# A weight pool of three buffers kept open to the end, and two projection weights taken into an earlier stream of weights

## The chip, the cores and the metric

The kernel runs on one core of one Trainium2 chip, as a single launch. The metric is its device time in microseconds (us), as the median of several runs. In the profile, PE is TensorE (PEld its weight loads), DVE is VectorE, ACT is ScalarE, POOL is GpSimd, and SP is SyncE, which here only issues DMAs. The "granted clock" is the share of TensorE's full clock that its throttle granted.

## The reference

One layer of a hybrid encoder block is applied to 1024 tokens (one prompt and one sample of 512 each), with a model width of 1024, all in float32:

```python
h    = rms_norm(x, norm_g)
proj = h @ w_in      # [cq 384 | ckv 256 | k_rope 64 | gate_a 1024 | conv_in 2*1024 | gate_c 1024 | mg_a 1024 | mg_c 1024]
# branch A: latent attention, 8 heads, 128 plain + 64 rotary dimensions per head
q    = rms_norm(cq) @ w_uq;  k_nope, v = split(rms_norm(ckv) @ w_ukv)
q, k = per-head rms_norm, rotary on the last 64
y_a  = (softmax(q k^T / sqrt(192)) v * silu(gate_a)) @ w_o_attn
# branch C: convolution
u    = conv_in[:, :1024] * sigmoid(conv_in[:, 1024:])
u    = depthwise_conv31(u) + dw_bias
u    = silu(layer_norm(u)) * silu(gate_c)
y_c  = u @ w_pw2     # the pointwise projection
out  = x + (sigmoid(mg_a) * y_a + sigmoid(mg_c) * y_c) @ w_out
```

## The kernel before

Activations lie transposed: the 128 partitions hold 128 channels, the free dimension holds tokens, in two halves of 512. The tokens' halves are the two groups of a PSUM block (128 x 1024).

**Weights as two parts.** Each float32 matmul is done as three matmuls in the faster type fp32r: high part by high part, high weight by low activation, low weight by high activation. So each weight block of 1024 x 128 (stored as 128 x 1024) goes through `load` (L112, a 512 KB DMA into a buffer `raw`, issued on SP) and `split` (L117): ACT casts it into `whi` (L128), and `whi` is subtracted from it into `wlo` (L129) by DVE or by POOL. Weights have running numbers: `raw46`, `whi46` and `wlo46` belong to weight 46, which is p0, the first block of the pointwise projection.

**Buffers.** Weights of the first part live in the pool `w1` with three buffers each of `raw`, `whi` and `wlo`, and so a new split waits until PE has read the one three before for the last time, and until that one's `wlo` has been made (which frees `raw`). The same pool holds four work tiles `s1` to `s4`. At L586 the pool is closed and a new one, `w`, is opened with two buffers each of `whi` and `wlo`, and one of `raw`.

**Order.** The program hands out instructions to the engines by priorities and buffers. PE's own order is written out in code in the first part. Each engine runs its instructions in the order it was handed, and each waits for semaphores of others; so what stands ahead of a waiting instruction on an engine delays it. Weights are prepared ahead, at a raised priority, by two functions. In the first part it is `ensure` (L162), which runs along a list `stream`: a block that is entry e of it calls `ensure(e + 3)`, so that three entries are prepared when it starts, and its low part is made on POOL:

```python
e = used[0]
ensure(e + 3)
ps = [one_bank(f"i{e}_{b}") for b in range(2)]
block_mm(ps, stream[e][0], hh, hl, (0, 1), ks=range(4))
between()
block_mm(ps, stream[e][0], hh, hl, (0, 1), ks=range(4, KD))
```

After that it is `prep` (L182), with the low part on DVE: `block(i)` (L331) does block i and then calls `prep(i + 2)`.

**Stages in order of time.** (1) 0 to 50 us: x is loaded, normalised and transposed into `hH`/`hL`. (2) to 434 us: most blocks of `h @ w_in`, in pairs with fewer products, while DVE does the depthwise convolution. (3) to 504 us, the tail: the last six gate blocks ga2 to ga7 (entries 72 to 77 of the stream, weights 40 to 45; PSUM tile `pbi`). Among them run the "tokens": eight groups of 128 tokens, each with a load of the convolution's output `yt` and of the saved gate `gt` (SP), eight transposes (PE), statistics and the inverse deviation `lrs` (DVE, the power on POOL, L248), the normalised `z` (DVE, L552), eight transposes of z (PE, L558), the activation `zs` (ACT, L561), a product with the gate (DVE), a cast into `cH` (ACT, L564) and the low part `cL` (DVE, L565). Each gate block is finished by `gate_out` (L479): two ACT instructions from PSUM into `stga` (L482), and a DMA issued on ACT. The code of the tail and of what follows it:

```python
tail = plan[len(plan) - NLN :]
with tc.manual_schedule(engines={nc.tensor.engine}):
    take(*tail[0], single())
    for n, u in enumerate(tail[1:]):
        tokens(2 * n)
        take(*u, single(lambda: tokens(2 * n + 1)))
```

(4) 507 to 594 us: the pointwise projection, blocks p0 to p7 (weights 46 to 53), on `cH`/`cL` as activations; DVE multiplies each by a saved gate `smc` (L608). (5) the latents (weights 54 to 58), the rotary key (59) and rotary weights (60), then the merge gates ma6 and ma7 (61 and 63) and the weights of the heads (h0 is 62, h1 64, h2 65 and so on). ma6 and ma7 end in `late_gate` (L858): two ACT instructions `stma` (L861), in front of the first of which ACT loads another function table. (6) to 977 us: attention, by heads. The weights of the second rotary group (`rawr1`, high part `wrh` at L976, low part `wrl` at L977) are loaded in the first heads. The first head's key goes through the casts `kh` (L794, low part `kl` on DVE) and `k1`/`k2` (L803), its query through `qsq` (L771) and `qh`, its rotary part through `qr` (L704) and `qrT` (L718). (7) to 1064 us: `w_o_attn`, blocks o0 to o7, merged with the saved gates `sma` (L1030), which `load_merge` (L1016) loads. (8) to the end: `w_out`, and y is written.

Of the kernel before, what the change touches and what calls it, by code (L numbers as in the profile page):

```python
# [9 lines left out]
F32 = mybir.dt.float32  # L10
# [7 lines left out]
P = 128  # L18
D = 1024
S = 512  # L20
NT = 1024
KD = 8
# [5 lines left out]
TAPS = 31  # L28
# [15 lines left out]
def encoder_block(tc, xp_d, xs_d, win_d, wkr_d, whd_d, wqr_d, wo_d, wp_d, wout_d, vec_d, dwk_d, rg_d, rc_d, yp_d, ys_d):  # L44
# [3 lines left out]
    def open_pool(name, **kw):  # L48
        if kw.get("space") is not DRAM:
            kw["reuse_waits"] = "tile"  # L50
        cm = tc.tile_pool(name=name, **kw)
        opened[name] = cm
        return cm.__enter__()

    def close_pool(*names):
        for name in names:
            opened.pop(name).__exit__(None, None, None)

    f = lambda ap: ap.bitcast(F32)
# [11 lines left out]

    cp = open_pool("const", bufs=1, side="left")
    wp = open_pool("w1", bufs=3, side="left")
    dr = open_pool("dr", bufs=1, space=DRAM)

    ep = open_pool("edge", bufs=1, side="right")
# [4 lines left out]
    p1 = open_pool("p1", bufs=2, space=PSUM)  # L81

    vec = cp.tile([P, NV], F32, name="vec")
    dwk = cp.tile([P, KD, TAPS], F32, name="dwk")
    rt = cp.tile([P, 4, 4, RD], F32, name="rt")
    identf = cp.tile([P, P], F32, name="identf")
    identr = cp.tile([P, P], F32R, name="identr")
# [1 line left out]
    fold = cp.tile([P, RD], F32, name="fold")  # L89
    mhalf = cp.tile([P, 8], F32, name="mhalf")  # L90
    gqk = cp.tile([P, 1], F32, name="gqk")
    ma_s = dr.tile([KD, P, NT], F32, name="ma_s")
    mc_s = dr.tile([KD, P, NT], F32, name="mc_s")
    ga_s = dr.tile([KD, P, NT], F32, name="ga_s")
# [9 lines left out]
    J = {}  # L104
# [5 lines left out]
    nraw = 3  # L110
# [22 lines left out]
    stream = []  # L133
# [3 lines left out]
    def sums(n, i1, i2):  # L137
        lo_, hi_ = slice(0, S), slice(S, D)
        if n == 0:
            for i in (i1, i2):  # L140
                if i not in wraw:
                    load(i)
        r1, r2 = wraw[i1], wraw[i2]
        t = lambda k: wp.tile([P, S], F32, tag=f"s{k}", bufs=1, name=f"s{k}_{i1}")
        if n == 0:
            s1, s2 = t(1), t(2)
            nc.gpsimd.tensor_add(s1, r2[:, lo_], r2[:, hi_])
            nc.gpsimd.tensor_add(s2, r1[:, lo_], s1)  # L148
            ssum[i1] = [s1, s2]
            return r1[:, lo_], s2  # L150
        s1, s2 = ssum[i1]
        if n == 1:
            s3 = t(3)
            nc.gpsimd.tensor_add(s3, r1[:, lo_], r2[:, lo_])  # L154
            return s3, s1
        if n == 2:
            s4 = t(4)
            nc.gpsimd.tensor_add(s4, r1[:, hi_], s2)
            return s4, r1[:, hi_]
        return (r2[:, hi_],)  # L160
# [21 lines left out]
    def prep(i, ahead=3000):  # L182
        if i < len(wjobs) and i not in wdone:
            with tc.high_priority(offset=ahead):
                if i not in wraw:
                    load(i)
                split(i)
# [35 lines left out]
    i = 0  # L223
# [58 lines left out]

    def combine_x(k):
        b11, b12, b21, b22 = (xw[kk, b] for kk in (k, k + 4) for b in range(2))
        t = {n: wp.tile([P, S], F32, tag=f"s{n}", bufs=1, name=f"t{n}_{k}") for n in (1, 2, 3, 4)}
        nc.gpsimd.tensor_sub(t[2], b12, b11)
        nc.scalar.copy(TH[1, k], t[2])
        nc.gpsimd.tensor_sub(TL[1, k], t[2], f(TH[1, k]))
        nc.gpsimd.tensor_sub(t[3], b12, b22)
        nc.gpsimd.tensor_sub(t[2], b22, t[2])  # L290
        nc.gpsimd.tensor_sub(t[4], b21, t[2])
        at_ = {2: (k + 4, 1), 3: (k, 1), 4: (k, 0)}
        TL[4, k] = tp.tile([P, S], F32R, tag=f"x{k + 4}_0", name=f"tL4_{k}")
        for n in (2, 3, 4):
            TH[n, k] = tp.tile([P, S], F32R, tag="x%d_%d" % at_[n], name=f"tH{n}_{k}")
            nc.scalar.copy(TH[n, k], t[n])
            nc.gpsimd.tensor_sub(TL[n, k], t[n], f(TH[n, k]))
# [100 lines left out]
    y = {}  # L398
# [71 lines left out]
    pb = open_pool("pb", bufs=6, space=PSUM)  # L470
# [105 lines left out]
            load_tok(t + 1)  # L576

    tail = plan[len(plan) - NLN :]
    with tc.manual_schedule(engines={nc.tensor.engine}):
        take(*tail[0], single())  # L580
        for n, u in enumerate(tail[1:]):
            tokens(2 * n)
            take(*u, single(lambda: tokens(2 * n + 1)))
    for i in range(4):
        nc.gpsimd.tensor_mul(rt[:, i], rc[:, i % 2], rg[:, i].unsqueeze(1).to_broadcast([P, 4, RD]))
    close_pool("z", "y", "s", "w1", "ln", "pb")  # L586
    pp = open_pool("pp", bufs=3, space=PSUM)
    p1 = open_pool("p1", bufs=2, space=PSUM)
    wp = open_pool("w", bufs=2, side="left")
    nraw = 1  # L590
    prep(J["p", 0])
    prep(J["p", 1])


    mp = open_pool("m", bufs=2, side="left")
# [268 lines left out]
    sq0, _, kv0 = latent("kv", 0, V_KL, 3)  # L864
    sq1, _, kv1 = latent("kv", 1, V_KL, 4)
# [18 lines left out]
    qsum, _ = latent("cq", 0, V_QL, 0, flat(pq0))  # L884
    for i in (1, 2):
        sq, _ = latent("cq", i, V_QL, i)
# [74 lines left out]
    for s_ in range(4 * NU + 3):  # L961
        n, j = divmod(s_, 4)
        if n < NU:
            h, b = units[n]
            if j == 0:
                if b == 1 and h + 2 < H:
                    prep(J["h", h + 2], 0)
                if n + 1 < NU:
                    load_gate(*units[n + 1])
                if h in (2, 3):  # L970
                    gr.append(rope_q(1, h - 2, b))
                if (h, b) == (1, 0):
                    raw = wp.tile([P, 6 * P], F32, tag="raw", bufs=1, name="rawr1")
                    wrope[1] = [ap_.tile([P, 6 * P], F32R, name=f"wr{x}", bufs=1) for x in "hl"]
                    nc.sync.dma_start(raw, wqr_d[1])
                    nc.scalar.copy(wrope[1][0], raw)  # L976
                    DVE.tensor_sub(wrope[1][1], raw, f(wrope[1][0]))  # L977
            prs[s_] = scores(h, b, j, res[n])
            if s_ == 0:
                next(ga[1])  # L980
            if j in (0, 2) and n + 1 < NU:
                res[n + 1] = next(ga[n + 1])
            if j == 3 and n + 2 < NU:
                ga[n + 2] = stage_a(*units[n + 2])
                next(ga[n + 2])
            if gr and next(gr[0], 0) == 0:
                gr.pop(0)
        q = s_ - 2
        if q >= 0:
            qn, qj = divmod(q, 4)  # L990
            if qj % 2 == 0 and q > 0:
                pn, pj = divmod(q - 1, 4)
                av(*units[pn], pj // 2, res[pn], *pts)
            if qn < NU:
                qh, qb = units[qn]
                if qj % 2 == 0:
                    pts = [ap_.tile([P, 4, 2 * P], F32R, tag="pt", name=f"pt{i}{q}", bufs=4) for i in range(2)]
                transp(qh, qb, qj, prs[q], *pts)
        if n == NU - 1:
            for u in units[3 * j : 3 * j + 3]:  # L1000
                split_attn(*u)
# [51 lines left out]
    for t in range(8):  # L1053
# [3 lines left out]
        for grp in ((0, 1),) if t < 7 else ((0,), (1,)):  # L1057
# [7 lines left out]
            o = fin.tile([P, D], F32, tag="o", name=f"o{t}_{grp[0]}")  # L1065
            DVE.tensor_add(o[:, cs], flat(ps)[:, cs], xr[:, cs])  # L1066
            nc.sync.dma_start(y_rows(t)[:, cs], o[:, cs])
    close_pool("fin", "wo", "me", "edge", "pp2", "dr", "w", "const")


_INS = ["x_prompt", "x_sample", "win", "wkr", "whd", "wqr", "wo", "wp", "wout", "vec", "dwk", "rg", "rc"]
# [69 lines left out]
```

## Time and profile before

| | us |
|---|---|
| three runs | 1154.6, 1154.98, 1158.98 |
| median | 1154.98 |
| profiled execution, time | 1157.69 |
| its span (first to last instruction) | 1155.9 |
| PE busy | 1126.9 |
| DVE, ACT, POOL busy | 772.1, 475.6, 420.1 |
| mean granted clock | 0.994 |

The profile shows one execution. Its time is 1.8 us longer than the span that the trace covers, and 2.7 us longer than the median of the runs. In a timeline row the columns are start and duration in us, engine, line, operation, output and inputs, shapes, and how many instructions are taken together; in brackets stands how long the engine was idle before, and what released it. Times of the stages above are from its timeline.

### The profile page before, as it was taken

Reading aid. Unit: us, or ns where it says so; the run is one execution under the profiler, and the core shown is the slowest. Engines: PE = TensorE matmul, PEld = TensorE weight load, DVE = VectorE, ACT = ScalarE, POOL = GpSimd, SP = SyncE. Lnnn points to the kernel's source line nnn. Section 1 sums busy time; section 2 is a strip of 40 time slices with the busy share of each in tenths; the row PEclk is TensorE's granted clock in tenths of the full one; section 3 lists DMA queues with packets and bytes.
Section 4 is the critical chain, followed back from the end, with each engine's and each line's share of the span. In section 5 each row is a group of like instructions: output and inputs, shape, how many; then the busy total and the mean of one; then the engine's idle time right before and its main releaser. Section 6 shows DMA issues by size and latency. Waiting matters only on the chain.

```text
span 1155.9 us, 15038 instructions
## 1 busy us (share of the span) xinstructions
PE 1126.9 (97%) x5796; PEld 956.4 (83%) x5796; DVE 772.1 (67%) x1123; ACT 475.6 (41%) x920; POOL 420.1 (36%) x359
## 2 busy tenths in 40 slices
PE   6899999999999999999999998999999999999998
PEld 4688888888888887878888887999999998888886
DVE  5599999999999986722214364778878887344311
ACT  6423334343334425630113245766677785112100
POOL 5969687878787843100000012222122211000000
PEclk9899999999999999999999999999999999999999
DMA  7012233132323356534341111100110101345331
GB/s 259 21 54 87 73 113 110 56 111 90 116 67 143 109 179 189 160 110 164 133 159 37 44 67 58 43 19 27 34 35 28 38 19 38 109 164 174 136 109 73
DMA packets 45352, 108.47 MB, mean 94 GB/s; under 512 B 3680, under 2 KB 19296, under 8 KB 45280
## 3 DMA queue, kind: packets, MB, share of 16 engines
q1 hardware_dynamic: 40384, 90.73, 23.7%
q10 hardware_dynamic: 4896, 16.78, 3.6%
q8 instruction: 45, 0.74, 0.3%
q14 instruction: 27, 0.22, 0.1%
HBM read 78.66 MB, written 28.84 MB: 93 GB/s over the span
## 4 chain that ended last, share of the span: by engine, by line
PE 91%; ACT 2%; DVE 1%; POOL 1%; DMA 0%; issue 0%; SPq 0%; ACTq 0%; DVEq 0%
PE blk L323 22%; PE pbi L323 11%; PE po L1063 8%; PE pbd L355 3%; PE pbb L355 3%; PE pba L355 3%; PE pba L354 3%; PE pbb L354 3%; PE pbd L354 3%; PE pbd L356 3%; PE pba L356 3%; PE pbb L356 3%; PE pt L830 2%; PE pkv L738 1%; PE pkv L739 1%; PE pkv L740 1%
## 5 line engine op out<-in xcount | busy, mean ns | idle before, releaser
L410 DVE SCALAR_TENSOR_TENSOR py<-u,dwk,py 128x1024 f32<-128x1024 f32 x224 | 288.4, 1287 | 5.7
L128 ACT CAST whi<-raw 128x1024 fp32r<-128x1024 f32 (+3 forms) x49 | 49.9, 1019 | 210.4 <-PE blk L323 166.4
L179 POOL TENSOR_TENSOR olo<-s,ohi 128x512 fp32r<-128x512 f32 x64 | 83.5, 1325 | 11.6 <-ACT ohi L178 11.5
L129 DVE TENSOR_TENSOR wlo<-raw,whi 128x1024 fp32r<-128x1024 f32 (+2 forms) x37 | 46.3, 1253 | 55.9 <-ACT whi L128 55.9
L323 PE MATMUL pbi<-hH,whi 128*128 128x512 f32 x192 | 76.7, 400 | 4.1 <-DVE u L498 4.1
L323 PE MATMUL pbi<-hL,whi 128*128 128x512 f32 x192 | 75.7, 394 | 0.0
L179 POOL TENSOR_TENSOR olo<-raw,ohi 128x512 fp32r<-128x512 f32 x48 | 63.3, 1319 | 26.1 <-ACT ohi L178 15.8
L248 POOL TENSOR_TENSOR rk<-sk,mhalf 128x4 f32<-128x4 f32 x16 | 17.2, 1074 | 147.5 <-DVE sk L748 122.1
L323 PE MATMUL blk<-a,whi 128*128 128x512 f32 x256 | 68.4, 389 | 0.0
L178 ACT CAST ohi<-raw 128x512 fp32r<-128x512 f32 x48 | 29.7, 620 | 88.0 <-POOL s L154 26.0
L821 ACT ACTIVATE pr<-sc,nm,sqs 128x512 f32<-128x512 f32 x64 | 51.2, 801 | 30.6 <-DVE nm L819 30.5
L323 PE MATMUL pbi<-hH,wlo 128*128 128x512 f32 x192 | 60.0, 394 | 0.0
L178 ACT CAST ohi<-s 128x512 fp32r<-128x512 f32 x64 | 38.1, 621 | 52.5 <-POOL s L148 29.4
L323 PE MATMUL blk<-hL,whi 128*128 128x512 f32 x144 | 57.2, 397 | 0.2 <-DVE hL L305 0.2
L323 PE MATMUL blk<-hH,whi 128*128 128x512 f32 x144 | 56.2, 398 | 1.1 <-ACT hH L304 0.7
L323 PEld LDWEIGHTS blk<-a,whi 128*128 128x128 f32 x256 | 48.0, 188 | 9.9
L608 DVE TENSOR_TENSOR tmc<-blk,smc 128x1024 f32<-128x1024 f32 x8 | 9.8, 1225 | 65.3 <-PE blk L323 65.3
L323 PE MATMUL blk<-cH,whi 128*128 128x512 f32 x128 | 50.5, 395 | 2.4 <-ACT whi L128 2.4
L1066 DVE TENSOR_TENSOR o<-po,xr 128x1024 f32<-128x1024 f32 (+1 forms) x9 | 10.0, 1106 | 63.9 <-PE po L1063 63.9
L248 POOL TENSOR_TENSOR rkv<-rkv,mhalf 128x8 f32<-128x8 f32 x1 | 1.6, 1647 | 133.8 <-DVE rkv L677 133.8
L323 PE MATMUL blk<-cL,whi 128*128 128x512 f32 x128 | 50.3, 393 | 0.0
L354 PE MATMUL pba<-hH,ohi 128*128 128x512 f32 x128 | 49.8, 389 | 0.0
(282 smaller groups left out, 3385.5 us busy)
## 6 DMA issues: line engine op xcount, KB each, us to landing
raw<-in_win_dram SPq DMA_DIRECT2D x53, 512.0 KB, 3.5
mc_s<-stmc ACTq DMA_DIRECT2D x8, 512.0 KB, 2.6
gc_s<-stgc ACTq DMA_DIRECT2D x8, 512.0 KB, 2.6
ga_s<-stga ACTq DMA_DIRECT2D x8, 512.0 KB, 3.9
gt<-gc_s SPq DMA_DIRECT2D x8, 512.0 KB, 4.4
raw<-in_wp_dram SPq DMA_DIRECT2D x8, 512.0 KB, 5.0
smc<-mc_s SPq DMA_DIRECT2D x8, 512.0 KB, 4.6
tc_s<-tmc SPq DMA_DIRECT2D x8, 512.0 KB, 3.0
```

The lines of the kernel that those rows point to most:

```text
L128: nc.scalar.copy(hv, rv)
L129: (sub or DVE).tensor_sub(lv, rv, f(hv))
L178: nc.scalar.copy(hi[:, sl], src)
L179: nc.gpsimd.tensor_sub(lo[:, sl], src, f(hi[:, sl]))
L323: mm(ps[b] if isinstance(ps, list) else ps[:, b], (wlo if wl_ else whi)[:, k], xl(k, b) if xl_ else xh(k, b), start=(k == 0 and wl_ == 0 a ...
L354: mm(ps, hi[:, k], xh, start=first and k == 0, stop=False, skip_group_check=not first)
L355: mm(ps, hi[:, k], xl, start=False, stop=False, skip_group_check=not first)
L356: mm(ps, lo[:, k], xh, start=False, stop=k == 3, skip_group_check=not first)
L410: DVE.scalar_tensor_tensor(out, u[:, :, i : i + S], dwk[:, j, i : i + 1], src, op0=ALU.mult, op1=ALU.add)
L821: ACT(pr, ps, AF.Exp, bias=nm, scale=r["sq"][:, j : j + 1], accum_out=sm)
L830: nc.tensor.transpose(pt[:, kt], pr[:, kt * P : (kt + 1) * P], identf)
L1063: mm(ps[:, n], lhs[k][:, ts_], w[k][:, n * S : (n + 1) * S], start=first_, stop=last_)
```

## The change

The pool `w1` stays open to the end, with its three buffers each of `raw`, `whi` and `wlo`; the second pool `w`, of two and one, is gone, and with it the two preparations of p0 and p1 at that place. The work tiles `s1` to `s4` and the convolution's kernel `dwk` move to a pool of their own, `k0`, which is closed where `w1` was. Two small tiles, `cpad` and `kpad`, hold no data and only move addresses. The first two weights of the pointwise projection become entries 78 and 79 of the stream, after entry 77, ga7: so the calls of `ensure` of ga6 and ga7 prepare weights 46 and 47, which before were prepared after the tail; the projection's first block p0 still calls `prep` for p2 (weight 48), and p1 for p3. The buffer of `rawr1` is one of the three raw buffers.

```diff
     wp = open_pool("w1", bufs=3, side="left")
+    k0 = open_pool("k0", bufs=1, side="left")
...
-    dwk = cp.tile([P, KD, TAPS], F32, name="dwk")
+    dwk = k0.tile([P, KD, TAPS], F32, name="dwk")
...
+    cp.tile([P, 120], F32, name="cpad")
+    k0.tile([P, 8], F32, name="kpad")
...
-        t = lambda k: wp.tile([P, S], F32, tag=f"s{k}", bufs=1, name=f"s{k}_{i1}")
+        t = lambda k: k0.tile([P, S], F32, tag=f"s{k}", bufs=1, name=f"s{k}_{i1}")
...
     tail = plan[len(plan) - NLN :]
+    stream += [(J["p", i],) for i in range(2)]
     with tc.manual_schedule(engines={nc.tensor.engine}):
...
-    close_pool("z", "y", "s", "w1", "ln", "pb")
+    close_pool("z", "y", "s", "k0", "ln", "pb")
     pp = open_pool("pp", bufs=3, space=PSUM)
     p1 = open_pool("p1", bufs=2, space=PSUM)
-    wp = open_pool("w", bufs=2, side="left")
-    nraw = 1
-    prep(J["p", 0])
-    prep(J["p", 1])
...
-                    raw = wp.tile([P, 6 * P], F32, tag="raw", bufs=1, name="rawr1")
+                    raw = wp.tile([P, 6 * P], F32, tag="raw", bufs=nraw, name="rawr1")
...
-    close_pool("fin", "wo", "me", "edge", "pp2", "dr", "w", "const")
+    close_pool("fin", "wo", "me", "edge", "pp2", "dr", "w1", "const")
```

The lines of the changed kernel are numbered three higher between its first additions and the tail, and as before from the pointwise projection on. Which instruction stands where on an engine follows from the program's scheduler. A row below is line, operation, output, inputs and shape, in the engine's order; the number at a name's end counts tiles and means nothing.

ACT at the end of the tail, from the last token's cast on, before:

```order
L564 CAST cH1_3486<-zs7_4140 128x8x128
L482 ACTIVATE stga7_4202<-pbi77_0_4152 128x512
L482 ACTIVATE stga7_4202<-pbi77_1_4153 128x512
L483 DMA ga_s_90<-stga7_4202 128x1024
L128 CAST whi46_4228<-raw46_4226 128x1024
L128 CAST whi47_4234<-raw47_4232 128x1024
L128 CAST whi48_4296<-raw48_4294 128x1024
```

And in the changed kernel:

```order
L567 CAST cH1_3491<-zs7_4151 128x8x128
L131 CAST whi48_4298<-raw48_4296 128x1024
L485 ACTIVATE stga7_4219<-pbi77_0_4169 128x512
L485 ACTIVATE stga7_4219<-pbi77_1_4170 128x512
L486 DMA ga_s_95<-stga7_4219 128x1024
L131 CAST whi49_4358<-raw49_4356 128x1024
L131 CAST whi50_4418<-raw50_4416 128x1024
```

The splits of weights 46 and 47 are gone from here: they stand further up, 46 between the casts of token 4 and the gate of ga5, 47 ahead of the gate of ga6. The split of 48 (p2) has moved to a place ahead of the two instructions of the gate of ga7.

POOL in the tail, from the low part of the last gate weight on, before:

```order
L129 TENSOR_TENSOR wlo45_3888<-raw45_3885,whi45_3887 128x1024
L248 TENSOR_TENSOR lrs4_3851<-lrs4_3851,mhalf_86 128x1
L248 TENSOR_TENSOR lrs5_3928<-lrs5_3928,mhalf_86 128x1
L248 TENSOR_TENSOR lrs6_4001<-lrs6_4001,mhalf_86 128x1
L248 TENSOR_TENSOR lrs7_4072<-lrs7_4072,mhalf_86 128x1
```

And in the changed kernel:

```order
L132 TENSOR_TENSOR wlo45_3893<-raw45_3890,whi45_3892 128x1024
L251 TENSOR_TENSOR lrs4_3856<-lrs4_3856,mhalf_89 128x1
L251 TENSOR_TENSOR lrs5_3933<-lrs5_3933,mhalf_89 128x1
L132 TENSOR_TENSOR wlo46_4043<-raw46_4040,whi46_4042 128x1024
L251 TENSOR_TENSOR lrs6_4006<-lrs6_4006,mhalf_89 128x1
L251 TENSOR_TENSOR lrs7_4083<-lrs7_4083,mhalf_89 128x1
L132 TENSOR_TENSOR wlo47_4166<-raw47_4163,whi47_4165 128x1024
```

The low parts of 46 and 47, which DVE made before, now stand on POOL, the first between the inverse deviations of tokens 5 and 6.

ACT around the gate of ma6 (`stma6`; `rsq` is a square of the rotary query), before:

```order
L696 ACTIVATE rsq0_1_0_5245<-pqr0_1_0_5226 128x512
L128 CAST whi62_5287<-raw62_5285 128x896
L696 ACTIVATE rsq0_1_1_5276<-pqr0_1_1_5257 128x512
L861 ACT_TABLE_LOAD
L861 ACTIVATE stma6_0_5346<-blk61_5291 128x512
L861 ACTIVATE stma6_1_5349<-blk61_5291 128x512
L128 CAST whi63_5342<-raw63_5340 128x1024
```

And in the changed kernel:

```order
L696 ACTIVATE rsq0_1_0_5247<-pqr0_1_0_5228 128x512
L131 CAST whi63_5344<-raw63_5342 128x1024
L696 ACTIVATE rsq0_1_1_5278<-pqr0_1_1_5259 128x512
L131 CAST whi64_5525<-raw64_5523 128x896
L861 ACT_TABLE_LOAD
L861 ACTIVATE stma6_0_5348<-blk61_5293 128x512
L861 ACTIVATE stma6_1_5351<-blk61_5293 128x512
```

The splits are one weight ahead: 64 instead of 62 is the one next to the table load, it now stands directly ahead of it, and 63 no longer follows the gate. Further on, `qsq` and `qh` of the first head stand ahead of its first casts `qrT` instead of behind two of them.

ACT around the gate of ma7 (`stma7`), before:

```order
L777 ACTIVATE ks0_0_5434<-pkv0_0_5373,rk0_0_5400 128x128
L704 CAST qr0_1_0_5518<-rt10_1_0_5247 128x8x64
L128 CAST whi64_5523<-raw64_5521 128x896
L861 ACTIVATE stma7_0_5527<-blk63_5439 128x512
L861 ACTIVATE stma7_1_5530<-blk63_5439 128x512
L794 CAST kh0_0_5549<-pkT0_0_5544 128x512
L803 CAST k10_0_5563<-pkr10_0_5553 128x512
```

And in the changed kernel:

```order
L704 CAST qr0_1_0_5520<-rt10_1_0_5249 128x8x64
L777 ACTIVATE ks0_0_5436<-pkv0_0_5375,rk0_0_5402 128x128 x4
L131 CAST whi65_5822<-raw65_5820 128x896
L861 ACTIVATE stma7_0_5529<-blk63_5441 128x512
L861 ACTIVATE stma7_1_5532<-blk63_5441 128x512
L976 CAST wrh_6063<-rawr1_6062 128x768
L794 CAST kh0_0_5551<-pkT0_0_5546 128x512
L803 CAST k10_0_5565<-pkr10_0_5555 128x512
```

The split next to the gate is that of 65 (h2) instead of 64 (h1), and the cast of the second rotary weights, `wrh`, has moved up to a place between the gate and `kh`; its low part `wrl` has likewise moved up on DVE, ahead of `kl`.

On SP, the loads `raw46`, `raw47`, `raw48` and `raw49` now stand among the tokens' loads (ahead of `yt2`, `gt3`, `gt5` and `gt7`), where before `raw46` followed `gt7`; `raw50` and `raw51` stand ahead of the first loads of `smc`. At the end of attention, the first loads of `sma` stand between the two gate loads of the last head instead of at 594.95 us.

More of the change, by code (lines that the diff above doesn't have):

```diff
@@ L284, in combine_x @@
         b11, b12, b21, b22 = (xw[kk, b] for kk in (k, k + 4) for b in range(2))
-        t = {n: wp.tile([P, S], F32, tag=f"s{n}", bufs=1, name=f"t{n}_{k}") for n in (1, 2, 3, 4)}
+        t = {n: k0.tile([P, S], F32, tag=f"s{n}", bufs=1, name=f"t{n}_{k}") for n in (1, 2, 3, 4)}
         nc.gpsimd.tensor_sub(t[2], b12, b11)
```

## The prediction, as it was put on record

> **What bounds the kernel now.** I read the page first, then the waits of PE, the timeline around PE's idle places, and stretches as windows.
>
> ```profile
> span 1155.9 us, 15038 instructions
> PE 1126.9 (97%) x5796; PEld 956.4 (83%) x5796; DVE 772.1 (67%) x1123; ACT 475.6 (41%) x920; POOL 420.1 (36%) x359
> ```
> ```profile
> PE blk L323 <- ACT whi L128: 2.4, 1, 2.4
> ...
> PE pqT L711 <- ACT qrT L718: 0.4, 1, 0.4
> ...
> PE blk L323 <- ACT qrT L718: 0.3, 1, 0.3
> ```
> ```profile
> 720.00:900.00 180.00, 179.80 (x1287) 166.91 (x1288) 143.35 (x375) 127.15 (x308) 41.58 (x42) 1.00 0.10 31
> ```
> The numbers of a wait are total, count and longest, in us; a window gives its length, the busy time of PE, PEld, DVE, ACT and POOL, the granted clock, the DMA share and GB/s. PE bounds nearly everything: 29 us of the span are left idle, and in the longest part of attention 0.2 of 180 us. So an edit counts only where PE waits. One such place lies where the change is: the first matmul of the pointwise projection.
>
> ```profile
> 503.40 0.39 PE L323 MATMUL pbi<-hL,whi 128*128 128x512 f32 x1
> 503.63 0.61 PE L323 MATMUL pbi<-hH,wlo 128*128 128x512 f32 x2
> 504.06 1.08 ACT L482 ACTIVATE stga<-pbi 128x512 f32<-128x512 f32 x2 [3.15 <-PE pbi L323]
> ...
> 505.59 1.04 ACT L128 CAST whi<-raw 128x1024 fp32r<-128x1024 f32 x1 [0.45 <-ACT stga L482]
> ...
> 506.69 0.80 PE L323 MATMUL blk<-cH,whi 128*128 128x512 f32 x1 [2.45 <-ACT whi L128]
> ...
> 509.42 0.49 PE L323 MATMUL blk<-cH,whi 128*128 128x512 f32 x1
> ```
> ```profile
> 506.00:509.00 3.00, 2.31 (x6) 1.83 (x7) 1.23 (x1) 0.64 (x1) 0.00 (x0) 0.54 0.52 187
> ```
> The last gate projection ends at 503.63 + 0.61 = 504.24. ACT then does the two halves of its gate, then p0's weight split, and p0's first matmul starts at 506.69, 0.06 after that split's end: a gap of 2.45 us. Behind it the clock is at half: six matmuls take 509.42 - 506.69 = 2.73 us, where the pitch at full clock is 503.63 - 503.40 = 0.23, so 1.38: 1.35 us more are lost. The place costs 3.80 us in all. That is the most that a cure of it could bring, 0.33% of the time.
>
> **Step A, the start of the pointwise projection.** With two entries more in the stream, the splits of p0 and p1 are made inside the token periods, p0's and p1's low halves on POOL instead of DVE. But the projection's first block calls for p2's split too, and on ACT this one now stands ahead of the last gate's two halves. It needs the buffer of the last gate projection's own weight, so it waits for that weight's last read by PE, the matmul at 503.40. And p0's first matmul, no longer waiting for a split, now waits for the second half of that gate, whose PSUM banks it reuses. One split is still in the way; it has changed places with the gate.
>
> ```profile
> 702.70 0.39 PE L323 MATMUL blk<-hL,whi 128*128 128x512 f32 x1
> ...
> 703.13 0.94 ACT L128 CAST whi<-raw 128x896 fp32r<-128x896 f32 x1 [8.21 <-PE blk L323]
> ...
> 703.98 1.08 ACT L861 ACTIVATE stma<-blk 128x512 f32<-128x512 f32 x2
> ```
> ```profile
> 463.27 1.05 ACT L128 CAST whi<-raw 128x1024 fp32r<-128x1024 f32 x1 [2.51 <-issue]
> ...
> 464.23 1.04 ACT L564 CAST cH<-zs 128x1024 fp32r<-128x1024 f32 x1
> 464.40 2.40 POOL L129 TENSOR_TENSOR wlo<-raw,whi 128x1024 fp32r<-128x1024 f32 x1 [4.36 <-ACT whi L128]
> ```
> The first fence has the same order elsewhere (last read, split, gate): the split starts 0.43 after the start of the read. So p2's split starts at 503.40 + 0.43 = 503.83, and the next ACT instruction 0.96 later (464.23 - 463.27), at 504.79; the gate's 1.08 end at 505.87, and PE starts 0.06 after, at 505.93. The gap is 1.69, the gain 0.76 us. The gap cannot be below 0.96 (the gate from 504.06 with nothing ahead of it ends at 505.14, PE starts at 505.20), a gain of 1.49; and it is above 2.45 only if the split starts after 504.59.
>
> Does the half clock behind the gap stay? Two other gaps bound it:
>
> ```profile
> 23.64 0.50 PE L323 MATMUL blk<-hH,wlo 128*128 128x512 f32 x1 [1.21 <-DVE rr L261]
> ```
> ```profile
> 24.00:28.00 4.00, 4.00 (x19) 3.28 (x18) 2.58 (x5) 2.67 (x6) 4.00 (x5) 1.00 0.72 188
> ```
> ```profile
> 706.16 0.51 PE L801 MATMUL pkr<-identr,kk 128*128 128x128 f32 x4 [1.88 <-ACT k L803]
> ```
> ```profile
> 707.00:711.00 4.00, 4.00 (x19) 3.75 (x18) 1.51 (x4) 2.81 (x6) 0.00 (x0) 0.57 0.37 132
> ```
> A gap of 1.21 left the clock at 1.00, one of 1.88 brought it to 0.57. 1.69 is nearer to 1.88, so I keep the loss of 1.35: nothing gained there (bounds 0 and -1.35).
>
> The Trainium skill, "TensorE: Matmul & The Clock Gate", section "HAM oscillation — how this bites in real kernels", warns of idle gaps of PE longer than some 3.4 us, the window of its activity monitor. Both gaps that lowered the clock here, 1.88 and 2.45, are shorter, so the trace does not agree with the Trainium skill's figure as a threshold. Read strictly, the Trainium skill's rule would keep the clock full behind 1.69, and the sum would be lower by the 1.35, as in rival 1.
>
> **The covers of the earlier splits** are costed at nothing. An ACT split fits into a token period (463.27, beside matmuls). On POOL the 2.40 of p0's low half go ahead of one token's inverse deviation, which the normalised z waits for:
>
> ```profile
> 482.43 1.34 DVE L552 TENSOR_SCALAR z<-yT,mv,lrs 128x1024 f32<-128x1024 f32 x1 [0.73 <-POOL lrs L248]
> ```
> ```profile
> 486.14 0.87 PE pbzT L558 x8
> ```
> ```profile
> 500.93 1.23 DVE L565 TENSOR_TENSOR cL<-zs,cH 128x1024 fp32r<-128x1024 f32 x1 [1.12 <-ACT cH L564]
> ```
> z ends at 483.77 and its transposes start at 486.14: 2.37 us of cover; without it, each us over is a us of PE. The last token ends at 502.16 and its cL is first read after 505.9. On SP the raw loads of p0 to p3 go into the token stage, each ahead of a token's gate load and waiting for an older low half; those after them go ahead of the first loads of the saved gates, which land later, as does the reload of the other gate at the end of attention:
>
> ```profile
> smc<-mc_s SPq DMA_DIRECT2D x8, 512.0 KB, 4.6
> ```
> ```profile
> L608 DVE TENSOR_TENSOR tmc<-blk,smc x8: 1224/1225/1225, 519.2 to 595.4; 128x1024 f32<-128x1024 f32 x8
> ```
> ```profile
> L1030 DVE TENSOR_TENSOR mm<-blk,sma x8: 1224/1225/1225, 988.6 to 1064.7; 128x1024 f32<-128x1024 f32 x8
> ```
> The first saved gate is needed at 519.2: issued even at 510, with 4.6 to landing, it is there. The other is needed at 988.6 and is now asked for between the two gate loads of the last head, which the SP queue shows as one row; with 4.6 to landing it has some 10 us in hand.
>
> ```profile
> 961.63 11.17 SPq L850 DMA_DIRECT2D sga<-ga_s  x2
> ```
> If one of these were late, DVE and then PE would wait for it for the missing time. With the pool of three kept, all later splits are made one weight earlier; where PE is at 179.8 of 180 us that is worth nothing, but at two places ACT's order decides.
>
> **Step B, the gate of ma7 and the first head.** The early split of h2 takes the place of h1's, the same price. But the rotary weight's cast of 768 columns now stands between the gate and the cast kh:
>
> ```profile
> 704.94 0.59 ACT L794 CAST kh<-pkT 128x512 fp32r<-128x512 f32 x1
> ...
> 705.56 0.69 DVE L795 TENSOR_TENSOR kl<-pkT,kh 128x512 fp32r<-128x512 f32 x1 [0.36 <-ACT kh L794]
> ```
> ```profile
> 721.13 0.92 ACT L976 CAST wrh<-rawr 128x768 fp32r<-128x768 f32 x1
> ```
> From 703.13 to 703.98 a cast of 896 columns holds ACT for 0.85; 768 columns make 0.73. kh, k and PE's 706.16 come later by that: +0.73, the gap 1.88 becomes 2.61. Where the cast was taken away (721), PE had no wait, so nothing comes back. Bounds: 0 (PE finds other work) and +1.2 (its low half, now ahead of kl on DVE, about as long as kl's 0.69 or somewhat more, comes last).
>
> **Step C, the gate of ma6.** h1's split now stands ahead of the table load and of the gate, and waits for a last read; the load was hidden before. The query square goes ahead of the transposed rotary casts.
>
> ```profile
> 678.85 1.28 ACT L861 ACT_TABLE_LOAD   x1
> ...
> 682.18 1.08 ACT L861 ACTIVATE stma<-blk 128x512 f32<-128x512 f32 x2 [2.05 <-PE blk L323]
> ...
> 683.54 1.05 ACT L128 CAST whi<-raw 128x1024 fp32r<-128x1024 f32 x1 [0.27 <-DMA raw<-in_win_dram]
> ...
> 684.49 0.61 ACT L704 CAST qr<-rt 128x512 fp32r<-128x512 f32 x1
> ...
> 689.21 0.65 ACT L718 CAST qrT<-pqT 128x256 fp32r<-128x256 f32 x2 [1.15 <-PE pqT L711]
> ```
> ```profile
> 689.75 0.62 ACT L771 ACTIVATE qsq<-pq 128x512 f32<-128x512 f32 x1
> ```
> Split (about 682.0, 0.85), load (1.28) and gate (1.08) end near 685.2 instead of 683.26, while the split at 683.54 has left: qr starts some 0.7 later than 684.49. Five us on, ACT had 1.15 of slack ahead of qrT, so this drowns, but qsq (0.62) and its partner now run first. PE's two waits on qrT are 0.4 and 0.3. If both go: -0.7; if both ACT steps come in full: +1.2. I take +0.4, a little over the middle, since PE's second transposes move behind other matmuls too.
>
> **Sum.** -0.76 + 0.73 + 0.4 = +0.37 us. The profiled execution took 1157.69 (span 1155.9 and 1.8 around it), 2.7 over the median of 1154.98; what I add does not depend on that. Profiled: 1158.1; median 1155.4.
>
> **Rivals.** (1) The clock stays full behind p0's shorter gap, as it did behind 1.21: another -1.35, 1154.0. For it: 1.69 lies between the two known gaps, and which of them it goes with is not shown; against it: it lies nearer to the one that lowered the clock, and the 2.45 of this very place did too. (2) The wait at p0 shrinks to the gate alone, because p2's split starts early or B and C find cover: gap 0.96 is -1.49, with the clock -1.35, B and C at 0: 1152.1. Against it: the split needs the last read at 503.40. With C at -0.7 it would be 1151.4, the lowest I can build. (3) Slower: at ma7 the gap of 2.61 keeps the clock at half longer. 707 to 711 ran at 0.57, a loss of 1.72; the same again is +1.72, so 1157.1. It decides if the gap reaches into another stretch in which the clock is judged. For it: PE already waited 1.88 there. With B and C at their upper ends (+0.47 and +0.8 more) it is 1158.3. (4) The change does not do what it says, the wait changes hands only: p2's split starts after 504.59, A is 0, time 1156.1; each us later is a us more.
>
> **How the numbers follow.** Forecast 0.45; (1) 0.22; (2) 0.08; (3) 0.13; (4) 0.07; something unseen 0.05. The likeliest gives 1155.4. The range runs from 1151.4, (2) with C's lower end, to 1158.5, a little above (3) with its upper ends. All the named cases lie inside; what is left out is for the unseen, and for the spread of single runs, which was 1154.6 to 1158.98 before. About 0.5%, 5.8 us, is what a measurement of this kernel can tell from no change; no case reaches it, so only the unseen and the spread of the runs stand there: faster 0.04, same 0.90, slower 0.06.
>
> **What would show it.** A: PE's wait ahead of p0 reads about 1.7 and is put down to the gate, ACT has p2's split at 503.8, and the window behind it has a clock near 0.54 (rival 1: 1.00). Token periods keep their length. B: PE waits some 2.6 for k near 707. C: the waits on qrT are 0.4 longer together. I am wrong if p0's gap lies outside 1.0 to 2.45, or if any new wait of over 1 us stands elsewhere on PE.

## The result, and the profile after

The changed kernel took 1159.49 us (median of 11 runs), the kernel before 1157.49 (11 runs, among them the three that the prediction started from). One of the changed kernel's runs took 1700.73 us at a mean granted clock of 0.62, and it is left out of the ratio and of what follows. The ratio is 1.0020, with a 95% interval of 1.0011 to 1.0029: some 2.3 us slower, where +0.4 was forecast. The median of 1154.98 from which the forecast was counted came from three runs that lay low; the profiled one, 1157.69, was close to what the kernel takes. The profile shown is of a run of 1160.44 us. Its page:

```profile
span 1158.7 us, 15045 instructions
...
PE 1131.0 (98%) x5796; PEld 960.6 (83%) x5796; DVE 763.2 (66%) x1121; ACT 475.2 (41%) x920; POOL 426.0 (37%) x361
```

PE is busy for 4.1 us more with the same 5796 matmuls, and idle for less (27.7 us instead of 29.0). So the loss is not in waits alone: matmuls took longer. The waits of PE after:

```profile
PE pkr L801 <- ACT k L803: 2.6, 1, 2.6
...
PE blk L326 <- ACT stga L485: 1.7, 1, 1.7
PE pqs L781 <- ACT qsq L771: 1.0, 1, 1.0
...
PE blk L326 <- ACT qrT L718: 0.3, 1, 0.3
```

Two of the three are as forecast: p0 waits 1.7 for the gate (forecast 1.69), the first key 2.6 (forecast 2.6). The wait of 1.0 for `qsq`, the square of the first query, is new: it is 1.02 us, and a new wait of over 1 us elsewhere on PE was one of the signs by which the prediction would be wrong. The timeline at p0 after:

```profile
504.57 0.39 PE L326 MATMUL pbi<-hL,whi 128*128 128x512 f32 x1
504.80 0.62 PE L326 MATMUL pbi<-hH,wlo 128*128 128x512 f32 x2
505.04 1.05 ACT L131 CAST whi<-raw 128x1024 fp32r<-128x1024 f32 x1 [1.85 <-PE pbi L326]
505.99 1.08 ACT L485 ACTIVATE stga<-pbi 128x512 f32<-128x512 f32 x2
...
507.12 0.50 PE L326 MATMUL blk<-cH,whi 128*128 128x512 f32 x1 [1.71 <-ACT stga L485]
507.46 0.40 PE L326 MATMUL blk<-cL,whi 128*128 128x512 f32 x1
```

p2's split starts 0.47 after the last read of the old weight, the gate follows 0.95 later, PE 0.05 behind the gate: the forecast chain, link by link. Behind it the matmuls follow at full pitch, while before they ran at half.

Where the clock is at half can be read off exactly, since the trace records the throttle: all stretches of half clock are 3.41 us long (or several of these; the last of a run is cut off by its end), and within one run they lie on one grid of 3.41 us, whose place against the program differs from run to run. In windows laid on that grid, each pair is one stretch and the one after it (columns as in the prediction). Before, around p0, the first query, and the second query of the first head:

```profile
502.79:506.20 3.41, 1.45 (x7) 0.87 (x5) 0.00 (x0) 1.69 (x3) 0.00 (x0) 1.00 0.07 28
506.21:509.62 3.41, 2.93 (x7) 2.35 (x8) 1.23 (x1) 0.43 (x1) 0.00 (x0) 0.50 0.51 162
687.11:690.52 3.41, 3.01 (x21) 2.43 (x19) 3.22 (x12) 2.23 (x7) 0.01 (x1) 1.00 0.33 114
690.53:693.94 3.41, 3.05 (x19) 2.56 (x20) 1.64 (x6) 3.41 (x13) 2.60 (x3) 1.00 0.00 0
...
717.83:721.24 3.41, 2.36 (x20) 1.97 (x20) 2.70 (x9) 3.41 (x10) 2.37 (x2) 1.00 0.20 75
721.24:724.65 3.41, 3.41 (x26) 3.21 (x25) 3.37 (x9) 2.28 (x6) 0.32 (x1) 1.00 0.10 14
```

After, at p0, the first query (step C), the first key (step B), and the second query:

```profile
504.16:507.57 3.41, 1.70 (x8) 1.12 (x7) 1.52 (x2) 2.03 (x3) 0.00 (x0) 1.00 0.00 0
507.57:510.98 3.41, 3.41 (x17) 2.78 (x16) 0.00 (x0) 0.00 (x0) 0.00 (x0) 1.00 0.90 269
688.48:691.89 3.41, 2.26 (x18) 1.76 (x16) 2.94 (x10) 2.90 (x10) 1.73 (x3) 1.00 0.00 0
691.89:695.30 3.41, 3.17 (x8) 2.50 (x9) 1.99 (x3) 2.80 (x9) 2.16 (x2) 0.50 0.00 0
705.55:708.96 3.41, 0.83 (x6) 0.83 (x7) 2.45 (x3) 2.72 (x6) 0.00 (x0) 1.00 0.67 201
708.96:712.37 3.41, 3.41 (x14) 3.07 (x14) 0.85 (x2) 2.45 (x4) 0.00 (x0) 0.50 0.63 226
719.20:722.61 3.41, 2.37 (x22) 1.99 (x21) 2.75 (x9) 3.41 (x10) 1.76 (x2) 1.00 0.46 133
722.61:726.02 3.41, 3.41 (x14) 2.93 (x13) 2.80 (x9) 2.15 (x5) 0.93 (x1) 0.50 0.00 0
```

The stretch behind p0 has the clock at 1.00 now. The one behind the first query is new at half: 8 matmuls in 3.17 us. The last pair shows chance: the stretch ahead has PE busy for 2.37 us after and 2.36 before, and the clock fell behind one and not behind the other, since the grid cuts the same instructions a little differently.

To say what each place costs I compare the start of the same matmul (the same count from the first) in the profile of a kernel and in that of before. The difference grows or shrinks mostly at a few places. The columns are: difference after 400 matmuls (107 us); its growth over p0 (504 to 552 us), over the first query (677 to 696), over the first key (703 to 711), over the second query (716 to 725); the ratio to before over all runs. All in us.

| kernel | start | p0 | first query (C) | first key (B) | second query | ratio, 95% interval |
|---|---|---|---|---|---|---|
| changed | +1.15 | -2.06 | +2.21 | +0.74 | +1.57 | 1.0020, 1.0011 to 1.0029 |
| pool alone | +1.60 | -2.06 | +2.24 | +0.76 | +1.56 | 1.0019, 1.0010 to 1.0028 |
| h1's split late | +2.14 | -2.06 | +1.35 | +0.74 | +1.54 | 0.9997, 0.9985 to 1.0008 |
| rotary cast late | +0.44 | -2.06 | +2.17 | 0.00 | -0.02 | 1.0005, 0.9996 to 1.0014 |
| gate first | +0.48 | -2.84 | +2.35 | +0.74 | 0.00 | 1.0013, 1.0002 to 1.0023 |
| three orders | -1.59 | -2.84 | +1.38 | -1.51 | -0.01 | 0.9983, 0.9974 to 0.9991 |
| four orders | -0.77 | -2.84 | +1.37 | -1.86 | +4.15 | 1.0000, 0.9988 to 1.0012 |
| changed, six matmuls | -0.92 | -2.04 | +0.75 | +0.72 | -0.01 | 0.9987, 0.9977 to 0.9998 |
| four orders, six matmuls | +0.45 | -2.84 | +0.61 | -1.85 | +3.03 | 0.9998, 0.9988 to 1.0007 |
| before, six matmuls | -0.22 | -0.99 | -0.01 | -1.52 | +1.44 | 1.0000, 0.9990 to 1.0009 |
| changed, two matmuls | +0.56 | -2.04 | +2.21 | +0.76 | +1.57 | 1.0030, 1.0019 to 1.0041 |
| two orders, six matmuls | -0.56 | -2.84 | +0.72 | +0.02 | +1.41 | 0.9987, 0.9977 to 0.9996 |
| two orders, four matmuls | -1.79 | -2.84 | +0.75 | -1.50 | +1.52 | 0.9993, 0.9982 to 1.0004 |

One row is one profiled run, the ratio is of 7 to 12 runs against 11 to 35 of before, so they need not add up. The start differs by -1.79 to +2.14 where the change does little: that is the run, not the kernel. The numbers come in steps: with and without a wait, and with and without a stretch of half clock (1.35 to 1.57 where PE has work all through).

Outside these columns the changed kernel gains 0.35 us, spread over 725 to 970 us. And the four kernels with the rotary cast late and h2's split not late (rotary cast late, three orders, both rows of two orders) lose a step of 0.78 us at the end of attention. There the first matmul of `w_o_attn` waits for DVE's product `attn`, which in the changed kernel it does not. In the changed kernel, and with the rotary cast late:

```profile
980.67 1.09 PE L326 MATMUL blk<-a,whi 128*128 128x512 f32 x4
```
```profile
978.34 1.20 PE L326 MATMUL blk<-a,whi 128*128 128x512 f32 x4 [0.52 <-DVE attn L846]
```

Each engine has the same order of instructions there; why the wait is new stays open. Three profiles (three orders, changed with six matmuls, two orders with four) also grow by 0.57 to 0.59 between 107 and 504 us, where the others stay within 0.07.

### The profile page after: what moved, and what is told of

Its sections match the earlier page's. It is cut to its first block, busy times and chain, and to the rows that moved or that the text cites. A ratio compares the mean times of both kernels' runs of the same rounds, so it can differ in the third digit from the quotient of the medians.

```text
span 1158.7 us, 15045 instructions
## 1 busy us (share of the span) xinstructions
PE 1131.0 (98%) x5796; PEld 960.6 (83%) x5796; DVE 763.2 (66%) x1121; ACT 475.2 (41%) x920; POOL 426.0 (37%) x361
## 4 chain that ended last, share of the span: by engine, by line
PE 90%; ACT 2%; DVE 1%; POOL 0%; DMA 0%; issue 0%; SPq 0%; ACTq 0%; DVEq 0%
PE blk L326 22%; PE pbi L326 11%; PE po L1063 8%; PE pba L358 3%; PE pbb L358 3%; PE pbd L358 3%; PE pbd L359 3%; PE pbb L359 3%; PE pba L359 3%; PE pba L357 3%; PE pbb L357 3%; PE pbd L357 3%; PE pt L830 2%; PE av L840 1%; PE pbc L358 1%; PE pbc L359 1%
## 5 line engine op out<-in xcount | busy, mean ns | idle before, releaser
L132 DVE TENSOR_TENSOR wlo<-raw,whi 128x1024 fp32r<-128x1024 f32 (+2 forms) x35 | 42.3, 1210 | 54.3 <-ACT whi L131 54.3
L359 PE MATMUL pbb<-tH,olo 128*128 128x512 f32 x128 | 49.9, 390 | 0.0
L357 PE MATMUL pbb<-tH,ohi 128*128 128x512 f32 x128 | 49.9, 390 | 0.0
```

The lines of the kernel that those rows point to most:

```text
L132: (sub or DVE).tensor_sub(lv, rv, f(hv))
L357: mm(ps, hi[:, k], xh, start=first and k == 0, stop=False, skip_group_check=not first)
L359: mm(ps, lo[:, k], xh, start=False, stop=k == 3, skip_group_check=not first)
```

## The experiments

My theory after the first comparison: the kept pool with its third buffer is the whole change; p0 gains 2.1 (0.75 of wait and a stretch of half clock), B loses 0.7, C loses 2.1, and the rest is where the grid falls. The rival: a loss spread over the program by addresses, loads or the start. In the edits `tc.issue_after(x.ins)` queues what its block issues on the engine of x behind x, with no wait for x to finish.

**The pool without the stream.**

```diff
-    stream += [(J["p", i],) for i in range(2)]
...
     p1 = open_pool("p1", bufs=2, space=PSUM)
+    prep(J["p", 0])
+    prep(J["p", 1])
```

> The pool of three kept, the two stream entries taken out, so that only the low halves of p0 and p1 go back from POOL to DVE. Theory (the pool's third buffer makes every early split and all three places): the same as the changed kernel, 2.3 us over before (1.3 to 3.3), with waits on PE of about 1.7 at p0, 1.0 at the first query's sums (qsq) and 2.6 at the first key (k). Rival (the entries of the stream, or POOL's 2.40 us splits, carry the loss): within 0.7 us of before or below it.

1159.52 us, ratio 1.0019, and the three waits are 1.7, 1.0 and 2.6:

```profile
PE pkr L802 <- ACT k L804: 2.6, 1, 2.6
...
PE blk L326 <- ACT stga L485: 1.7, 1, 1.7
PE pqs L782 <- ACT qsq L772: 1.0, 1, 1.0
```

ACT, SP and PE issue the same rows as in the changed kernel; even without the entries, the third buffer lets the raised priority put p0's and p1's splits into the tail. The stream's entries only decide whether DVE or POOL makes two low parts, and that costs nothing. The rival on them falls. Whether it is the third buffer of the raw weights, that of their two parts, or that the pool is never closed, was not separated.

**h1's split behind the gate of ma6 (C).**

```diff
-            ACT(st, ps[:, b * S : (b + 1) * S], AF.Sigmoid)
+            late[j] = ACT(st, ps[:, b * S : (b + 1) * S], AF.Sigmoid)
...
-    prep(J["h", 1])
+    with tc.issue_after(late[6].ins):
+        prep(J["h", 1])
```

> The split of h1 is issued behind the gate of ma6 instead of ahead of its table load. Theory (step C costs 2.0: the wait on qsq and a stretch of half clock behind it): 2.0 us below the changed kernel, so within 1 us of before, the wait on qsq under 0.5 us and no half clock near 692. Rival (the loss is spread over the program, by addresses, loads or the start): no change against the changed kernel, 2.3 us over before.

1158.01, ratio 0.9997: 2.3/1000 below the changed kernel's ratio, as expected, and the wait on `qsq` is gone from the list. In the profile the place costs 0.86 us less (2.21 to 1.35); the rest of the fall is not at it. But the profiled run has half clock near 692 all the same, against what I wrote:

```profile
689.01:692.42 3.41, 2.99 (x25) 2.48 (x24) 2.75 (x9) 3.39 (x11) 2.04 (x3) 1.00 0.00 0
692.42:695.83 3.41, 3.41 (x9) 2.62 (x9) 0.86 (x2) 2.30 (x7) 1.87 (x2) 0.50 0.08 18
```

PE is busy for 2.99 of 3.41 us ahead of it. So idle time alone is not what lowers the clock; this stretch holds transposes and the eight sums of one column each. The granted clock of this kernel's 12 runs goes from 0.991 to 0.999, that of the changed kernel's ten from 0.991 to 0.994. That would fit a place that falls badly in some runs and no longer in all, but it is not shown: the two other profiles with h1's split late and no added matmuls (three and four orders) have half clock there too.

**The rotary cast behind the key casts (B).**

```diff
-        nc.scalar.copy(r["k2"], f(pT2))
+        r["last"] = nc.scalar.copy(r["k2"], f(pT2))
...
-                    nc.scalar.copy(wrope[1][0], raw)
+                    with tc.issue_after(res[1]["last"].ins):
+                        nc.scalar.copy(wrope[1][0], raw)
```

> The cast of the second rotary weights is issued behind the first two heads' key casts instead of ahead of the first. Theory (step B costs 0.7 to 1.0): the wait on k goes back from 2.6 to 1.9, 0.7 to 1.0 us below the changed kernel, some 1.5 us over before. Rival of a spread loss: no change, 2.3 over before. Rival that a longer gap there costs a stretch of half clock more: 2.7 below the changed kernel.

1158.23, ratio 1.0005. The wait is back at its old size, and the place costs 0.00 instead of 0.74:

```profile
PE pkr L801 <- ACT k L803: 1.9, 1, 1.9
```

(The `res[1]` of the edit is the second half of the first head, not a second head.) The runs fell by 1.3 to 1.7, more than the wait, and less than with a stretch of half clock more (2.7): between the two expectations, and the interval holds the first and just reaches the second. By places it is not the wait alone either: what this one gives back at the first key, 0.74, is lost again at the end of attention, 0.78. What is left is the clock, and here the second query does not fall to half, and the mean granted clock of the runs is 0.9937 instead of 0.9927.

**The gate ahead of p2's split (A).**

```diff
-            ACT(st[:, b], ps[b], AF.Silu if nm[0] == "g" else AF.Sigmoid)
+            last_gate[0] = ACT(st[:, b], ps[b], AF.Silu if nm[0] == "g" else AF.Sigmoid)
...
-        ps = block(J["p", j], lambda k, b: cH[b][:, k], lambda k, b: cL[b][:, k])
+        with tc.issue_after(last_gate[0].ins):
+            ps = block(J["p", j], lambda k, b: cH[b][:, k], lambda k, b: cL[b][:, k])
```

> The split of p2 is issued behind the last gate's two halves. Theory: PE's wait ahead of p0 falls from 1.7 to about 1.0, 0.7 us below the changed kernel, some 1.6 us over before, the clock behind it full. Rival (p0 has another wait close behind the gate, cL or p0's low half): the wait stays over 1.3 and the time does not move.

1158.44, ratio 1.0013, as expected. The wait is the gate alone (0.95 us in the timeline, where the prediction gave 0.96 as the least), and p0 gains another 0.78:

```profile
PE blk L326 <- ACT stga L485: 0.9, 1, 0.9
```

**All three together**, the same edits:

> The three reorderings together (gate ahead of p2's split, h1's split behind the gate of ma6, rotary cast behind the key casts). Theory that the three places add up: 0.8 + 2.0 + 1.1 below the changed kernel, so 1.6 us below before (0.6 to 2.6). Rival (the places share a cost, such as stretches of half clock that the first gap decides): the best of the three alone, 0 to 0.5 below before.

1155.88, ratio 0.9983: 1.6 below the 1157.47 of before on that chip, as the sum said. It has the lowest ratio of the kernels tried (two with added matmuls, at 0.9987, have intervals that overlap with its own), and is the only one whose interval lies below 1 by its order alone. That the sum came out is in part luck: in the profile the first query still has its stretch at half (+1.38) and 0.78 is lost at the end of attention, while the first key's stretch stayed at full clock (-1.51), which the sum did not name.

**h2's split late, too**: `prep(J["h", h + 2], 0)` put into `tc.issue_after(res[0]["last"].ins)`.

> As the three orders, and the split of h2 is issued behind the first head's key casts. Theory: the wait on k falls by that split's 0.85, from 1.9 to about 1.05: 2.4 below before; if the clock stays full behind it, 3.8 below. Rival (the split is then missed where h2 is first used, or the next table load comes later): no lower than with the three orders.

1157.02, ratio 1.0000: the rival. The first key's place is better by 0.35 more, but the second query loses 4.15. There the late split now stands on ACT, PE waits 1.3 for `kk`, and two stretches of half clock follow:

```profile
PE pkr L801 <- ACT kk L762: 1.3, 1, 1.3
```

**Six idle matmuls in the changed kernel.** Ahead of the sums of the first query's squares, into their own PSUM bank, which the sums then overwrite:

```diff
+        if fill:
+            with tc.issue_after(last_q.ins):
+                for _ in range(6):
+                    mm(full, qh_w[:, 0], lat["cq", 0, 0, b], start=True, stop=True)
```

> The changed kernel, with six matmuls of 512 columns more, whose result is overwritten, between the rotary transposes and the sums of the first query's squares, where PE waits 1.0 us for the square. Theory (what lowers the clock behind that place is how few columns PE streams in a stretch of 3.4 us, idle or not): 0.36 us longer there, but no half clock near 692: 1.3 - 0.36 = 0.9 below the changed kernel, 1.3 over before. Rival (the clock falls for another reason than PE's load, or the wait alone is the cost): 0.4 above the changed kernel.

1155.98, ratio 0.9987: with more work, 3.5 us less than the changed kernel. At the place itself the loss went from 2.21 to 0.75 (0.9 less was expected, 1.46 came; with four matmuls the place costs the same 0.75, so the six take no time of their own there), and no stretch next to it is at half:

```profile
686.22:689.63 3.41, 3.41 (x28) 3.06 (x26) 2.94 (x10) 2.15 (x7) 1.07 (x2) 1.00 0.00 0
689.63:693.05 3.42, 3.12 (x17) 2.40 (x16) 1.84 (x5) 3.42 (x12) 2.76 (x3) 1.00 0.00 1
```

The other 2 us I cannot place. The mean granted clock of the runs is 0.9964 instead of 0.9927, two and a half stretches fewer, of which the place explains one. Whether the others are the start and the second query falling better in these twelve runs, or follow from the first, was not settled.

**The same six with the four orders, and in the kernel before:**

> The four orders and the six matmuls. Theory: where h1's split is late the wait on the square is under 0.2, so the six cost 1.2 us in full, and what they save is the half clock of the runs in which a stretch falls badly, up to 1.3: no change against the four orders within 0.7 us, with a narrower spread of the runs. Rival: 1.2 slower.

1156.48, ratio 0.9998: no change against the four orders, as expected; in its profile the place is at full clock and the second query still pays for h2's split (+3.03).

> The kernel before, with the same six matmuls at the first query's squares. Theory (they help only where that place runs into a stretch of half clock, which before it did in some runs only): PE waits 0.7 us there, so the six cost 0.7 and save up to 0.3 in the mean: 0.2 to 0.8 over before. Rival (the six help for another reason, by what they shift later): 1 to 3 below before, as in the changed kernel.

1156.6, ratio 1.0000. The interval (0.9990 to 1.0009) holds the theory's 0.2 to 0.8 us over and leaves out most of the rival's 1 to 3 below. So the six matmuls are no gain in themselves. This profile also shows that before did not lose its stretch behind p0 in every run: here the grid cut that gap in two, the clock stayed full, and p0 took 0.99 less than in the first profile. The first key's stretch stayed full too (-1.52).

**Two matmuls instead of six** (`range(2)`):

> The changed kernel with two such matmuls instead of six. Theory (a stretch that streams less than about a third of what PE could is followed by half clock): that stretch goes from 0.13 of its columns to 0.25, which is still below the 0.26 that was always followed by half clock: half clock near 692, no change against the changed kernel, 2.3 over before. Rival (any matmul that breaks the idle time is enough): as with six, 1.5 below before.

1160.01, ratio 1.0030. PE is busy for 2.83 of 3.41 us now, and the clock falls all the same, as the theory had it:

```profile
687.91:691.32 3.41, 2.83 (x21) 2.03 (x19) 2.94 (x10) 2.86 (x9) 1.69 (x3) 1.00 0.00 0
691.32:694.73 3.41, 3.13 (x7) 2.48 (x8) 2.04 (x3) 2.85 (x9) 2.21 (x2) 0.50 0.00 0
```

**Gate first, rotary cast late, and six or four matmuls:**

> The changed kernel with the gate ahead of p2's split, the rotary cast behind the key casts, and the six matmuls. Theory that the parts add up: 1.5 below the changed kernel with the six matmuls, so 3.0 below before (2.0 to 4.0). Rival (the key's wait of 1.9 and its stretch of half clock take the rest): 1.5 below before, as with the six alone.

1154.97, ratio 0.9987 (0.9977 to 0.9996): 1.5 below before by the ratio, the rival's number. The place behaves (+0.72), p0 and B are as in the single runs, but in this profile the second query is at half (+1.41), and the mean clock of the runs is 0.9957 against 0.9964 with the six matmuls alone. The parts do not add up in the mean, since what is gained in waits meets a count of stretches that the grid decides.

> As the last, with four matmuls, which fit into the wait of 1.0 and cost nothing, but leave the stretch at 0.38 of its columns, just above the highest that was followed by half clock. Theory: half clock near 692 in some of the runs at most; 3.0 to 3.4 below before. Rival (a share under 0.4 is not enough): half clock in most runs, 2.0 below before.

1155.74, ratio 0.9993 (0.9982 to 1.0004): less than expected. The runs fall into two groups, seven of 1154.4 to 1155.8 with the clock at 0.996 or 0.997, and five of 1158.0 to 1159.2 at 0.994, which is what half clock in some of the runs looks like; the profile is of the first group, and the place is at full clock in it. Which place falls in the second group is not shown.

## Why the prediction was wrong, point by point

**The base.** Of the 4.1 us between 1155.4 and 1159.49, 2.5 are the kernel before itself, 1157.49 in 11 runs instead of 1154.98 in three. The profiled run, 2.7 over that median, was left aside. This step alone put the time outside the range: counted from 1157.49, the range's upper end would be 1161.0 instead of 1158.5. The other 1.6 is the error of the sum: +2.0 between the medians (+2.3 by the ratio) instead of +0.37.

**Step A** had the right chain (1.69 forecast, 1.71 measured), and that one split still stands in the way. The term for the clock was the wrong one: I kept the half clock, and it was rival 1 that came: -2.06 in the profile instead of -0.76. That the stretch is a gain of 1.33 there is luck of the first profile of before: in the run with before's order and six matmuls elsewhere p0 was at full clock, and against it the change gains 1.07. Behind the changed kernels' gap of 1.7 or less none of the 12 profiles shows half clock. Interpolating a gap's length between 1.21 and 1.88 was the wrong measure; what the clock follows in these runs is how much PE streams in the stretch of the grid in which the gap lies. The 1.7 us at p0 have full matmuls on both sides in the same stretch.

**Step B** had the right wait: +0.73 forecast, +0.74 measured, 0.00 with the cast taken away. In the first two profiles one stretch of half clock followed the gap before and after, so rival 3 seems not to have come. Over all the profiles it did in part: behind a wait of 2.6 the stretch is at half in all six, behind one of 1.9 in three of six (among them one of the two with before's order), behind 1.5 in neither of two. So the longer wait seems also to make certain a loss that before came in some runs only; the profiles are few, and the sum had no term for it.

**Step C** is the term of the sum that failed: +0.4 forecast, with bounds of -0.7 and +1.2, and +2.21 measured. I had the order right (split, table load and gate ahead of `qr`, `qsq` ahead of `qrT`), but looked for the delay at `qrT` and let it drown in the slack there. It came out at `qsq`, whose buffer is freed by a DVE sum that hangs on the same late ACT chain, as these rows of after show:

```profile
688.99 0.60 ACT L771 ACTIVATE qsq<-pq 128x512 f32<-128x512 f32 x1 [1.46 <-DVE sk L746]
...
689.63 1.05 PE L781 MATMUL pqs<-ones,qsq 128*128 128x1 f32 x8 [1.02 <-ACT qsq L771]
```

That is 0.8 of wait, within the bounds. The other 1.35 to 1.4 is the stretch of half clock behind it, which the bounds did not hold, because I gave the clock a price at p0 and in rival 3 and none at this place. With h1's split late the wait went and the profiled run still paid 1.35: so these are two terms.

**The second query** (+1.57 in the profile) was not in the forecast, and the change does not touch it: in some profiles it costs that, in others nothing; with before's own order and six matmuls elsewhere it cost 1.44, in before's first profile nothing.

**The covers** held: the token periods and the saved gates' loads cost within 0.1 us (0.01 from 107 to 504 us, -0.08 from 552 to 677), and from 725 us on the changed kernel gains 0.35.

**Over all runs**, the time lost to the clock, (1 - mean granted clock) x time, is 5.7 us in 35 runs of before (0.9951) and 8.5 in ten of the changed kernel (0.9927). That difference of 2.8 is larger than the whole loss. So the change made PE wait about as much as before, and made the clock fall more often, and in every run: before's runs reach from 0.993 to 0.999, the changed kernel's only from 0.991 to 0.994. How the 2.3 us divide over the places in the mean of the runs stays open: the four places add up to 2.46 against the first profile of before, and to 3.54 against the one with the six matmuls.

## What to carry to other kernels

Where one engine is busy for 97%, a reordering elsewhere is worth its waits plus the clock that follows each wait; give every place that PE waits at, or fills with transposes and sums of one column, both prices, with and without. A deeper pool does not only start work earlier: every early split is put ahead of something on its engine, and where that something is a chain's link, queueing it behind keeps the gain and loses much of the price (the three orders: 0.9983 instead of 1.0020), though it can cost elsewhere, as the 0.78 at the end of attention. And take the base from the spread of the runs, not from three of them.

## What the runs showed of the hardware

The clock's stretches are 3.41 us long, on one grid per run. For each stretch between 55 and 1146 us in the 14 profiles that was itself at full clock, I took the columns streamed in it by matmuls and transposes as a share of 8192 (16 matmuls of 512), each counted from its start at full pitch. Of 20 stretches with a share below 0.28, all 20 were followed by half clock; of 15 from 0.28 to 0.37, 7 were; of 59 from there to 0.5, none. The two limits are not sharp: with each matmul counted wholly where it starts they are 0.31 and 0.38, and where it ends 0.25 and 0.44. Transposes have to be counted: 8 stretches that kept full clock lie below the highest share that lost it, and without the transposes 116 do. How long PE counts as busy says little: 2.99 of 3.41 us was followed by half clock, 1.70 at p0 was not. At the first query the share was 0.13 in the changed kernel, 0.25 with two matmuls more, and 0.59 with six. So outside these limits a rule of columns fits all the profiles, and the clock behind the first query with six and with two matmuls was forecast by it; no edit tried it at another place.

The Trainium skill, "TensorE: Matmul & The Clock Gate", section "HAM oscillation — how this bites in real kernels", speaks of gaps over some 3.4 us. The length of the grid agrees with that figure. But here a stretch with a gap of 1.0 us was enough, and so was one in which PE's pauses add up to only 0.42 us.
